# Second-half LRU in the RWKV slots, and two streams of RWKV recurrences in one PSUM bank

## The chip, the cores and the metric

One core of one Trainium2 chip runs the whole program. The metric is the device time of one execution in microseconds (us). Five engines work from queues of their own: TensorE (PE), VectorE (DVE), ScalarE (ACT), GpSimd (POOL) and SyncE (SP). An engine takes its instructions in the order in which they stand in its queue, so an instruction that waits holds up all that is behind it.

## The reference, cut to what matters

One layer of a hybrid recurrent network, for a prompt of 1024 tokens and 8 single-token samples, in float32:

```python
xn = _rmsnorm(x, norm1_g)
P = xn @ w_in                                  # 1024 x 3456, columns split among three groups
o_r, S_r = _rwkv7(...)                         # 6 heads of 64; S = S*diag(w) - ... + v k^T, token by token
o_h, S_h = _hgrn2(...)                         # 6 heads of 64; gated linear attention in chunks of 64
o_l, h_l, c_l = _rglru(...)                    # 256 channels; width-4 convolution, h = a*h + b
x = x + concat([o_r, o_h, o_l]) @ w_out
x = x + square(relu(_rmsnorm(x) @ mlp_w1)) @ mlp_w2
y = _rmsnorm(x)
```

All final states are outputs too. Within `_rwkv7` the last steps are a group norm of each head (mean, variance, scale), a bonus term and a gate.

## The kernel before, in words

Channels lie on the 128 partitions, tokens along the free dimension. The prompt is worked in two halves of 512 tokens (`hf` 0 and 1; the 8 samples ride with half 1).

**The dense products.** Each float32 weight matrix is split into a high and a low part (`wh`, `wl`), and so are the activations (`xh`, `xl`), and a dense tile is 24 matmuls: 8 blocks of 128 rows, three products each. `projections()` is one long generator that makes the dense tiles one after another: the input projection of half 0, tiles `in_...` of 512 tokens, that of half 1 in pieces of 256 and 264, then `out_proj(0)`, `out_proj(1)` and the first part of the MLP. The order of the column blocks is `ORDER`: r, w, l, h are the blocks of RWKV (r, k, v), of its low-rank parts, of the LRU and of HGRN; in half 1 it is `w0 r0 h0 r1 r2 h1 h2 l0 l1`. The up and down products of the MLP come after that and fill the second half of the run.

**The recurrences.** RWKV is worked in 12 parts `q`: a pair of heads `j`, a half `hf`, a quarter `qt` of 256 tokens, that is four chunks of 64 (`PARTS`). A part goes through `rw_operands` (exponentials, transposes), `rw_inverse` (a triangular inverse, matmuls `sc`, `W` and `Y`), `rw_chain` (for each chunk three dependent small matmuls into the tile `ch`, named `pa`, `pu` and `pst` in the code, each read by DVE before the next; at the end 24 small matmuls `po` for the outputs of the part) and `rw_finish` (the group norm on ACT and DVE, then transposes `oT` and the matmul `gate`). HGRN is `hg_run` with its matmuls `hvT`, `hqk`, `gram`, `hkT`, `hS`, `ho`, `hoT`, and for the samples `hsrow`, `hso`, `hsq`; `rw_sample` does the RWKV samples. The LRU is `lru` with the matmuls `lg`.

**What sets the order.** Only PE's order is made by hand. `weave` runs the generators against a planned clock `now`: a generator yields either a number (so many us until its next piece is due; these are the constants D1 to D42) or a key that another one must have set. At each turn the recurrence whose piece is due goes first, and the dense generator fills what is left. The order of the other engines is made by the framework's scheduler, with the priorities of `PRI`.

**Slots.** The projection writes its results into SBUF slots. There are `RPM` = 6 slots "pm" for the r, k, v tiles of RWKV, freed when the operands of the second quarter are done, and `HPM` = 8 slots "hpm" for HGRN (four tiles a block) and the LRU (two tiles a block, `xb` and `gl`). `take` holds the dense generator until a slot is free. The third work tile of the LRU, `lq`, is one buffer of its own. The slots "pm" are taken again by `out_proj`, for the residual tiles `xr` (loaded by POOL's DMA queue) and for squares.

**PSUM banks.** Eight banks: "big" 2 for the dense tiles, "ra" 2 for the inverse, "ch" 1 for the chain and its outputs, "o" 1 shared by all other small products of RWKV and LRU, "h" 2 for HGRN. `bank_o` and `used_o` keep planned time between two uses of "o".

Of the kernel before, what the change touches and what calls it, by code (L numbers as in the profile page):

```python
# [37 lines left out]
L_EV, L_OPS, D1, D2, D3, D4, D5, D6, D7, D8, D9, D10, D11, D12, D13, D14, D15, D16, D17, D18, D19, D20, D21, D22, D23, D24, D25, D26, D27, D28, D29, D30, D31, D32, D33, D34, D35, D36, D37, D38, D39, D40, D41, D42, L_N0, L_RB, L_O = 1.59, 2.88, 3.2, 10.6, 3.9, 1.6, 1.6, 1.6, 6.4, 1.6, 0.5, 1.6, 4.5, 2.08, 2.6, 1.6, 1.6, 1.8, 1.6, 3.8, 8.5, 1.6, 1.5, 3, 1.45, 2, 3, 0.8, 2, 2.6, 4, 4, 4, 1.6, 1.6, 6.31, 1.6, 3.3, 3, 0.99, 9.63, 1.6, 2.2, 1.1, 7.82, 0.54, 1.6  # L38
# [4 lines left out]
PRI = [-100, 0, 0, 300, 300, 300, 100, 300]  # L43
# [9 lines left out]
def kernel(ctx: ExitStack, tc: tile.TileContext, i, o):  # L53
# [397 lines left out]

    def shifted(hf, col, name, out, tag, bufs):
# [3 lines left out]
        pm = rwp.tile([P, HW], F32, tag=tag, name=f"pm_{name}", bufs=bufs)  # L456
# [69 lines left out]
    def rw_operands(q):  # L526
# [49 lines left out]
        G.memset(ee[:, :, 0:1], 1.0)  # L576
        act(ee[:, :, 1:C + 1], ck(t2), AF.Exp)
        act(t1, t2, AF.Exp, scale=-1.0)
        V.tensor_copy(wc, ee[:, :, C])
# [44 lines left out]
    def rw_inverse(q):  # L624
# [7 lines left out]
        sa, ym, xm, mv, kv = (w2(nm, n, u).rearrange("p (u t) -> p u t", t=C) for nm, u in (("sa", 2), ("ym", 3), ("xm", 2), ("mv", 3), ("kv", 3)))  # L632
# [971 lines left out]
```

## Time and profile before

| | us |
|---|---|
| median of 3 timed runs | 1579.41 |
| lowest, highest | 1573.84, 1581.77 |
| the profiled execution, its own time | 1583.56 |
| the profiled execution, first to last instruction (span) | 1581.8 |
| PE busy | 1500.9 |
| DVE, ACT, POOL busy | 757.3, 665.3, 382.5 |

The profile is one execution. "Idle before, releaser" is the time that an engine stood still just ahead of an instruction, and what ended it. A row of the timeline has the start in us, the duration, the engine, the line, the operation, output and inputs, shapes, and the count of like instructions that are merged. Fp32 matmuls whose operands are not split appear as two records each (x16 for 8 matmuls). PE's durations overlap: the pitch of a stream of matmuls is the difference of their starts, not their duration. PEclk is the clock that PE was granted, as a share of full speed.

Up to about 620 us the input projection and the recurrences of both halves run side by side, from about 686 us the first tiles of `out_proj(0)` run beside what is left of the recurrences, and from about 860 us on the MLP has PE to itself.

### The profile page before, as it was taken

What the parts mean: (1) busy time and instruction counts of PE and PEld (TensorE: products, weight loads), DVE (VectorE), ACT (ScalarE), POOL (GpSimd) and SP (SyncE); (2) the same over time, 40 slices, a digit from 0 to 9 for tenths busy, and PEclk for the clock granted to TensorE, in tenths of its full rate; (3) what the DMA queues carried; (4) which work ended last, traced back from release to release, by engine and by line L of the source; (5) the groups of instructions that cost most, each with busy time, mean ns of one, the idle gap of its engine ahead of it and who ended that gap; (6) DMA issues with size and microseconds to landing.
All of it is one profiled execution on the core that took longest, in us unless ns stands there. A gap on an engine that the chain in (4) does not pass through costs nothing.

```text
span 1581.8 us, 31488 instructions
## 1 busy us (share of the span) xinstructions
PE 1500.9 (95%) x13112; PEld 1322.7 (84%) x13112; DVE 757.3 (48%) x1799; ACT 665.3 (42%) x1433; POOL 382.5 (24%) x531
## 2 busy tenths in 40 slices
PE   8989999999998899978999999999999999999997
PEld 6767777888898888866798899889898989988887
DVE  7777866756566665574555222222222222222224
ACT  4544656546544556255434324232332323233232
POOL 4553323224335324323312110101111010101011
PEclk9989999998999999799999999999999999999999
DMA  4334334344434334235442544535344454544242
GB/s 152 125 68 96 84 81 94 79 83 98 91 75 96 74 81 91 62 73 124 119 128 81 107 80 99 102 83 104 83 104 83 102 92 85 102 86 101 47 93 108
DMA packets 53086, 146.98 MB, mean 93 GB/s; under 512 B 6960, under 2 KB 7248, under 8 KB 52944
## 3 DMA queue, kind: packets, MB, share of 16 engines
q0 software_dynamic: 22976, 65.33, 24.9%
q1 hardware_dynamic: 29824, 79.61, 16.1%
q8 instruction: 103, 1.69, 0.5%
q14 instruction: 39, 0.32, 0.1%
q10 hardware_dynamic: 144, 0.04, 0.0%
HBM read 138.87 MB, written 6.07 MB: 92 GB/s over the span
## 4 chain that ended last, share of the span: by engine, by line
PE 72%; DVE 10%; issue 6%; ACT 5%; DMA 4%; POOL 2%; POOLq 0%; SPq 0%; DVEq 0%; ACTq 0%
PE up L76 22%; PE dn L76 19%; PE in L76 13%; PE out L76 4%; PE ch L76 2%; PE W L76 2%; PE Y L76 2%; PE sc L76 1%; PE gram L76 1%; DMA wl_out<-in_w_out 1%; DVE rq L1035 1%; PE ho L76 1%; DMA raw_in<-in_w_in 1%; DMA wl_w<-in_w 1%; ACT gsq L768 1%
## 5 line engine op out<-in xcount | busy, mean ns | idle before, releaser
L76 PE MATMUL in<-xl,wh_in 128*128 128x512 f32 (+3 forms) x648 | 223.4, 345 | 2.1 <-DVE xl L385 2.1
L76 PE MATMUL in<-xh,wh_in 128*128 128x512 f32 (+3 forms) x648 | 223.9, 345 | 0.0
L76 PE MATMUL dn<-hh,wl_w 128*128 128x264 f32 (+2 forms) x696 | 223.2, 321 | 0.3 <-DMA wl_w<-in_w 0.2
L76 PE MATMUL dn<-hh,wh_w 128*128 128x264 f32 (+2 forms) x696 | 222.8, 320 | 0.0
L76 PE MATMUL dn<-hl,wh_w 128*128 128x264 f32 (+2 forms) x696 | 222.7, 320 | 0.0
L76 PE MATMUL in<-xh,wl_in 128*128 128x512 f32 (+3 forms) x648 | 221.4, 342 | 0.5 <-DVE wl_in L293 0.3
L1492 DVE TENSOR_TENSOR mix<-mix,dn 128x512 f32<-128x512 f32 (+2 forms) x192 | 98.4, 512 | 243.4 <-PE dn L76 243.4
L296 POOL DMA_DIRECT2D wl_w<-in_w x86 | 75.2, 877 | 575.4 <-ACT hh L1422 305.9
L291 ACT ACTIVATE wh_w<-raw_w 128x512 fp32r<-128x512 f32 (+1 forms) x90 | 70.7, 785 | 281.6 <-PE dn L76 228.0
L1421 DVE SCALAR_TENSOR_TENSOR rl<-up,rl 128x512 f32<-128x512 f32 (+2 forms) x96 | 49.5, 516 | 204.5 <-ACT rl L1420 204.4
L76 PE MATMUL up<-nxh,wh_w 128*128 128x264 f32 (+1 forms) x512 | 145.9, 285 | 0.1
L76 PE MATMUL up<-nxl,wh_w 128*128 128x264 f32 (+1 forms) x512 | 145.0, 283 | 0.5 <-POOL nxl L1318 0.5
L76 PE MATMUL up<-nxh,wl_w 128*128 128x264 f32 (+1 forms) x512 | 145.3, 284 | 0.0
L76 PEld LDWEIGHTS dn<-hh,wl_w 128*128 128x128 f32 x696 | 130.8, 188 | 14.1 <-DMA wl_w<-in_w 4.4
L76 PEld LDWEIGHTS dn<-hl,wh_w 128*128 128x128 f32 x696 | 130.9, 188 | 10.1
L76 PEld LDWEIGHTS dn<-hh,wh_w 128*128 128x128 f32 x696 | 131.0, 188 | 9.3
L76 PEld LDWEIGHTS in<-xl,wh_in 128*128 128x128 f32 x648 | 127.4, 197 | 13.4 <-DVE xl L385 4.2
L76 PEld LDWEIGHTS in<-xh,wl_in 128*128 128x128 f32 x648 | 127.1, 196 | 11.1 <-issue 1.0
L76 PEld LDWEIGHTS in<-xh,wh_in 128*128 128x128 f32 x648 | 127.3, 196 | 10.6 <-issue 0.7
L1420 ACT ACTIVATE rl<-up 128x512 f32<-128x512 f32 (+2 forms) x96 | 43.3, 451 | 141.0 <-PE up L76 140.9
L76 PE MATMUL up<-nl,wh_w 128*128 128x512 f32 x256 | 101.5, 397 | 0.0
L76 PE MATMUL up<-nh,wl_w 128*128 128x512 f32 x256 | 101.5, 396 | 0.0
(461 smaller groups left out, 3328.3 us busy)
## 6 DMA issues: line engine op xcount, KB each, us to landing
raw_in<-in_w_in SPq DMA_DIRECT2D x53, 512.0 KB, 3.4
wl_in<-in_w_in POOLq DMA_DIRECT2D x43, 512.0 KB, 5.7
raw_w<-in_w SPq DMA_DIRECT2D x32, 512.0 KB, 3.5
raw_w<-in_w SPq DMA_DIRECT2D x64, 256.0 KB, 2.7
wl_w<-in_w POOLq DMA_DIRECT2D x58, 256.0 KB, 4.1
wl_w<-in_w POOLq DMA_DIRECT2D x28, 512.0 KB, 5.6
raw_out<-in_w_out SPq DMA_DIRECT2D x16, 512.0 KB, 3.5
out_y_prompt<-yt SPq DMA_DIRECT2D x16, 256.0 KB, 2.0
```

Of the source, the lines that this page charges most:

```text
L76: PE.matmul(out, lhsT, rhs, start=start, stop=stop)
L291: act(wh[:, ks], raw[:, ks], AF.Copy)
L296: G.dma_start(wl[:, ks], src[:, ks], accum_op=ALU.add)
L768: act(sq, raw[:, g * 64:(g + 1) * 64], AF.Square, bias=sums[:, 0, g:g + 1], accum_out=sums[:, 1, g:g + 1])
L1035: V.tensor_tensor(qp[g][hp, h, :], qef[hp, gc], q[hp, gc], op=ALU.mult)
L1420: act(rl[:, :n], pt[:, :n], AF.Relu)
L1421: V.scalar_tensor_tensor(rl[:, :n], pt[:, :n], 0.0, rl[:, :n], op0=ALU.max, op1=ALU.mult)
L1492: V.tensor_tensor(x2[m][:, c0:c0 + n], x2[m][:, c0:c0 + n], pt[:, :n], op=ALU.add)
```

## The change

- The LRU of half 1 takes its tiles from the slots "pm", after RWKV's r, k and v, and the third work tile (`gq`, before `lq`) is a slot too: three "pm" a block in half 1, three "hpm" a block in half 0.
- `rw_chain` runs as two streams. The pairs (quarter 0 and 1 of one pair of heads) go to them in turn: parts 0, 1, 4, 5, 8, 9 to one, 2, 3, 6, 7, 10, 11 to the other. Each stream has its own `az`, `yz`, `rh`, `ws` and state buffers, and uses its own half of one tile `ch`, made once, in the bank "ch". `bank_ch` and `used_ch` keep 0.9 us of planned time between two chain matmuls of either stream.
- The 24 output matmuls of a part go to a tile `po` in the shared bank "o", held for 3.5 us of planned time, and wait for the previous part's finish before they start, not after.
- To find the room in SBUF: the tile `ee` is gone (`ar` holds the exponentials first and is multiplied in place; a third, shifted Exp per part on ACT), the tile `raw` is gone (the outputs go to one half of `ot`; the scaling is eight DVE instructions of 64 columns in place of four of 128), and `ym` has two buffers in place of three.

```diff
-PRI = [-100, 0, 0, 300, 300, 300, 100, 300]
+PRI = [-100, -100, 0, 0, 300, 300, 300, 100, 300]
...
+    ch_busy = [0.0]
+    def bank_ch():
+        while now[0] < ch_busy[0]:
+            yield ch_busy[0] - now[0]
+    def used_ch():
+        ch_busy[0] = now[0] + L_CH
...
+    def pm_tile(name):
+        return rwp.tile([P, HW + 3], F32, tag="pm", name=name, bufs=RPM)
...
-        G.memset(ee[:, :, 0:1], 1.0)
-        act(ee[:, :, 1:C + 1], ck(t2), AF.Exp)
+        G.memset(ar[:, :, 0, 0:1], 1.0)
+        act(ar[:, :, 1, :], ck(t2), AF.Exp)
         act(t1, t2, AF.Exp, scale=-1.0)
-        V.tensor_copy(wc, ee[:, :, C])
+        act(ar[:, :, 0, 1:C], ck(t2)[:, :, 0:C - 1], AF.Exp)
+        V.tensor_copy(wc, ar[:, :, 1, C - 1])
...
+    chb = ps("ch", "ch")
     def rw_chain(q):
...
         yield ("B", q)
+        if hf == 1 and qt == 0:
+            yield ("C", q - 5)
+        z = q // 2 % 2
+        az, yz = azs[z], yzs[z]
...
-        pt = ps("ch", f"ch_{n}")
-        pa, pu, pst = (pt[:, u * C:u * C + C] for u in range(3))
-        po = pt[:, QT:2 * QT]
+        pa, pu, pst = (chb[:, z * QT + u * C:z * QT + u * C + C] for u in range(3))
...
             if st is not None:
+                yield from bank_ch()
                 mm(pa, az[:, c].rearrange("p h t -> p (h t)"), st)
+                used_ch()
...
             if c == NQ - 1:
+                if q >= 1:
+                    yield ("N", q - 1)
+                po = (yield from bank_o(f"po_{n}"))[:, 0:QT]
                 for c_, h, b, cc in units():
...
-                if q >= 1:
-                    yield ("N", q - 1)
+                used_o(3.5)
...
                 for g in range(NQ):
-                    act(raw[:, g * 64:(g + 1) * 64], po[:, g * 64:(g + 1) * 64], AF.Copy, accum_out=sums[:, 0, g:g + 1])
+                    act(ot[:, g, 0], po[:, g * 64:(g + 1) * 64], AF.Copy, accum_out=sums[:, 0, g:g + 1])
...
         for g in range(NQ):
-            V.tensor_scalar(ot[:, g], bc(raw[:, None, g * 64:(g + 1) * 64], [P, 2, C]), sums[:, 0, g:g + 1], sums[:, 1, g:g + 1],
-                            op0=ALU.add, op1=ALU.mult)
+            for h in (1, 0):
+                V.tensor_scalar(ot[:, g, h], ot[:, g, 0], sums[:, 0, g:g + 1], sums[:, 1, g:g + 1], op0=ALU.add, op1=ALU.mult)
...
-        for w in ("xb", "gl"):
-            yield from take("hpm")
-            x.append(hp_tile(f"l{w}{t}_{hf}"))
-        xb, gl = x
+        for w in ("xb", "gl", "gq"):
+            yield from take("pm" if hf else "hpm")
+            x.append((pm_tile if hf else hp_tile)(f"l{w}{t}_{hf}"))
+        xb, gl, gq = x
...
-        gq = hgp.tile([P, HW], F32, tag="lq", name=f"lq{t}_{hf}", bufs=1)
...
-        free["hpm"] += 2
+        free["pm" if hf else "hpm"] += 3
...
-        weave([each(rw_chain, *NP), each(rw_inverse, *NP[0::2]), ...
+        weave([each(rw_chain, *(x for x in NP if x[0] // 2 % 2 == 0)), each(rw_chain, *(x for x in NP if x[0] // 2 % 2)), each(rw_inverse, *NP[0::2]), ...
```

What the change does to PE's order shows best near the end of half 1's input projection. In the rows, `ch` are chain matmuls, `W` and `Y` those of the inverse, `oT` and `gate` the finish of part 9, `hoT`, `hsrow`, `hso` and `hsq` the end of HGRN's block 1, and `in_1_...` the dense tiles. Before, on PE, the 52 rows that start with the `W` behind the last matmul of block h2 hold no dense matmul; these are the last 10 of them, and the first matmul of block l0 behind them:

```order
L76 MATMUL W_2_1_1_8129<-xm_1_1_7737,sa_1_1_7735 64x64 x8
L76 MATMUL hsrow_8139<-hsdg_8122,bones 128x512
L76 MATMUL ch_1_0_8118<-rh_2_1_0_8126,yz 128x64
L76 MATMUL Y_2_1_1_8146<-ym_1_1_7736,wm_2_1_1_8128 64x64 x8
L81 MATMUL oT_1_1_8157<-ident,ot_1_1_8077 128x128 x4
L76 MATMUL ch_1_0_8118<-mv_1_0_7011,bt_1_0_6811 128x64
L76 MATMUL gate_1_1_8170<-pm_xg_3608,gup 128x256
L76 MATMUL hso_8173<-hq_1_6529,hsst_8120 64x1 x16
L76 MATMUL W_2_1_1_8194<-xm_1_1_7737,sa_1_1_7735 32x32 x8
L76 MATMUL hsq_8205<-hssq_8191,bones 128x8
L76 MATMUL in_1_0_8242<-xh_3295,wh_in_1_7797 128x256
```

In the changed kernel, on PE at the same place, where `hoT` of HGRN's block 1 stands:

```order
L76 MATMUL ch<-st_1_184,az_187 128x64
L76 MATMUL in_1_256_7970<-xh_3268,wh_in_1_7520 128x264
L76 MATMUL in_1_256_7970<-xl_3276,wh_in_1_7520 128x264
L76 MATMUL Y_2_1_1_8024<-ym_1_1_7826,wm_2_1_1_7981 64x64 x8
L81 MATMUL hoT_1_8035<-ident,hot_1_7935 128x128 x4
L76 MATMUL ch<-st_1_1_1_7974,az_186 128x64
L76 MATMUL in_1_256_7970<-xh_3268,wl_in_1_7521 128x264
L76 MATMUL in_1_256_7970<-xh_3269,wh_in_1_7520 128x264
L76 MATMUL in_1_256_7970<-xl_3277,wh_in_1_7520 128x264
L76 MATMUL in_1_256_7970<-xh_3269,wl_in_1_7521 128x264
L76 MATMUL in_1_0_8061<-xh_3262,wh_in_1_7756 128x256
```

The last tile of h2 (`in_1_256_7970`) and the first of l0 (`in_1_0_8061`) now run on between the small matmuls, and l0 no longer stands behind `hsq`. Part 10 (`az_187`) and part 9 (`az_186`), of different streams, have chain matmuls between each other. This is the only longer place where they do: over all 12 parts the stream changes 11 times from one chain matmul to the next, seven of them here. From the last tiles of the input projection on (both kernels start `out_0` at the same row of PE's order, 3280) the two orders have the same pieces at nearly the same rows.

On POOL, the residual tiles `xr` of `out_proj` take "pm" slots. Before, the first two loads stand far ahead, between chain steps of half 1's first pair of heads:

```order
L735 TENSOR_SCALAR ws_0_1_1_6468<-st_0_1_1_6320,wc_1_1_5063 128x64
L736 TENSOR_TENSOR ws_0_1_1_6468<-ws_0_1_1_6468,kv_1_1_5292 128x64
L1260 DMA xr_0_8775<-in_xt 128x512
L861 DMA out_s_wkv<-s_st_6185 128x512
L1260 DMA xr_0_8923<-in_xt 128x512
L735 TENSOR_SCALAR ws_0_1_1_6598<-st_0_1_1_6467,wc_1_1_5063 128x64
```

In the changed kernel, on POOL, the second and third of them stand beside the last chain steps of part 11 (`ws_2_1_1`) and the first LRU output (`out_lru`):

```order
L1003 TENSOR_TENSOR kq_2_1_8980<-kq_2_1_8980,hf_1_7004 128x8x32
L306 DMA wl_out_0_8957<-in_w_out 128x1024
L1284 DMA xr_0_8962<-in_xt 128x512
L758 TENSOR_SCALAR ws_2_1_1_9108<-st_2_1_1_9017,wc_1_1_7591 128x64
L759 TENSOR_TENSOR ws_2_1_1_9108<-ws_2_1_1_9108,kv_1_1_7829 128x64
L1237 DMA out_lru<-lso_8505 128x36
L1284 DMA xr_0_9040<-in_xt 128x512
```

The loads now come after the LRU of half 1 has had the slots; the second one (`xr_0_8962`) waits for a DVE result.

More of the change, by code (lines that the diff above doesn't have):

```diff
@@ L455, in shifted @@
         pr = rwp.tile([P, HT + 16], F32, tag="praw", name=f"praw_{name}", bufs=1)
-        pm = rwp.tile([P, HW], F32, tag=tag, name=f"pm_{name}", bufs=bufs)
+        pm = pm_tile(f"pm_{name}") if tag == "pm" else rwp.tile([P, HW], F32, tag=tag, name=f"pm_{name}", bufs=bufs)
         def evac(pt, c0, n):
@@ L504 @@
     kz = rwp.tile([P, 2, NQ, 2, C], F32, name="kz")
-    az = rwp.tile([P, NQ, 2, C], F32, name="az")
-    yz = rwp.tile([P, NQ, 2, C], F32, name="yz")
+    azs, yzs = ([rwp.tile([P, NQ, 2, C], F32, name=f"{nm}{z}") for z in range(2)] for nm in ("az", "yz"))
     for h in range(2):
-        for z in (kz[brow[1 - h], 0, :, h], kz[brow[1 - h], 1, :, h], az[brow[1 - h], :, h], yz[brow[1 - h], :, h]):
-            G.memset(z, 0.0)
+        for z in (kz[:, 0], kz[:, 1], *azs, *yzs):
+            G.memset(z[brow[1 - h], :, h], 0.0)
     PARTS = [(j, hf, qt) for hf in range(2) for j in range(3) for qt in range(2)]
@@ L631, in rw_inverse @@
         sr = rwp.tile([P, 2, NQ, C], F32, tag="sr", name=f"sr_{n}", bufs=3)
-        sa, ym, xm, mv, kv = (w2(nm, n, u).rearrange("p (u t) -> p u t", t=C) for nm, u in (("sa", 2), ("ym", 3), ("xm", 2), ("mv", 3), ("kv", 3)))
+        sa, ym, xm, mv, kv = (w2(nm, n, u).rearrange("p (u t) -> p u t", t=C) for nm, u in (("sa", 2), ("ym", 2), ("xm", 2), ("mv", 3), ("kv", 3)))
         (S.copy if q < 2 else G.tensor_copy)(ym, bc(id64[:, None, :], [P, NQ, C]))
@@ L763, in rw_finish @@
         om = mix[j][:, hf * HT + qt * QT:hf * HT + qt * QT + QT]
-        ot, raw, sums, bo = (live[q][x] for x in ("ot", "raw", "sums", "bo"))
+        ot, sums, bo = (live[q][x] for x in ("ot", "sums", "bo"))
         V.tensor_scalar(sums[:, 0], sums[:, 0], -1.0 / 64.0, None, op0=ALU.mult)
@@ L767, in rw_finish @@
         for g in range(NQ):
-            act(sq, raw[:, g * 64:(g + 1) * 64], AF.Square, bias=sums[:, 0, g:g + 1],
+            act(sq, ot[:, g, 0], AF.Square, bias=sums[:, 0, g:g + 1],
                 accum_out=sums[:, 1, g:g + 1])
@@ L1250, in evac @@
             else:
-                sq = rwp.tile([P, HW], F32, tag="pm", name=f"sq{m}_{c0}", bufs=RPM)
+                sq = pm_tile(f"sq{m}_{c0}")
                 act(sq[:, :cn], xm, AF.Square)
@@ L1258, in load @@
             ws[m] = next_w(m + 1 < lead or m >= lead)
-            xts[m] = rwp.tile([P, HW], F32, tag="pm", name=f"xr{m}_{hf}", bufs=RPM)
+            xts[m] = pm_tile(f"xr{m}_{hf}")
             nc.gpsimd.dma_start(xts[m][:, :n], i["xt"][m * P:(m + 1) * P, s0:s0 + n])
@@ L1428, in norms @@
     def norms():
-        yield from norm2(*CH[0], lambda nm: rwp.tile([P, HW], F32, tag="pm", name=nm, bufs=RPM))
+        yield from norm2(*CH[0], pm_tile)
         for c in CH[1:]:
@@ L1435 @@
         dense_work = projections()
-        weave([each(rw_chain, *NP), each(rw_inverse, *NP[0::2]), each(rw_inverse, *NP[1::2]), each(rw_operands, *NP), each(rw_finish, *NP), hgrn(),
+        weave([each(rw_chain, *(x for x in NP if x[0] // 2 % 2 == 0)), each(rw_chain, *(x for x in NP if x[0] // 2 % 2)), each(rw_inverse, *NP[0::2]), each(rw_inverse, *NP[1::2]), each(rw_operands, *NP), each(rw_finish, *NP), hgrn(),
                each(lru, *((t, hf) for hf in range(2) for t in range(2)))], dense_work)
```

22 lines of the change are left out of this document (12 added, 10 removed).

## The prediction

> **What bounds the kernel now.** I read the busy times and the 40 slices of the page first, then windows of 20 us, then PE's own timeline where the windows dip, then PE's waits.
>
> ```profile
> span 1581.8 us, 31488 instructions
> PE 1500.9 (95%) x13112; PEld 1322.7 (84%) x13112; DVE 757.3 (48%) x1799; ACT 665.3 (42%) x1433; POOL 382.5 (24%) x531
> PE   8989999999998899978999999999999999999997
> PEclk9989999998999999799999999999999999999999
> ```
>
> PE is the bound: it stands still for 80.9 of 1581.8 us. The change issues the same matmuls, so it can win only where PE stands still or runs at a lower clock. In the second half (the MLP) both are almost absent. The one slice with a clock of 7 is the seventeenth, 633 to 672 us. Windows there (columns: PE, PEld, DVE, ACT, POOL busy, PE's clock, DMA share, GB/s):
>
> ```profile
> 600.00:620.00 20.00, 19.91 (x272) 18.41 (x271) 11.19 (x28) 10.60 (x20) 6.97 (x13) 1.00 0.41 80
> 620.00:640.00 20.00, 15.63 (x252) 12.85 (x250) 11.18 (x34) 9.65 (x45) 11.22 (x15) 0.80 0.35 86
> 640.00:660.00 20.00, 20.00 (x159) 18.27 (x158) 9.26 (x29) 3.26 (x7) 7.24 (x10) 0.68 0.19 44
> 660.00:680.00 20.00, 19.08 (x234) 17.79 (x234) 12.35 (x38) 11.62 (x33) 5.90 (x8) 1.00 0.40 89
> 680.00:700.00 20.00, 17.49 (x180) 14.13 (x179) 18.35 (x40) 12.78 (x27) 5.20 (x7) 1.00 0.18 54
> ```
>
> From 620 to 660 PE stands still for 4.4 us and loses a fifth and a third of its clock. PE's timeline shows what the stretch is made of:
>
> ```profile
> 620.40 0.28 PE L76 MATMUL in<-xh,wl_in 128*128 128x264 f32 x1
> 620.61 0.68 PE L76 MATMUL W<-xm,sa 64*64 64x64 f32 x16
> 621.59 1.15 PE L76 MATMUL ho<-vt,att 64*64 64x64 f32 x32
> 622.66 1.20 PE L76 MATMUL ho<-hst,rq 128*64 128x64 f32 x32
> ...
> 629.54 0.63 PE L81 MATMUL hoT<-ident,hot 128*128 128x128 f32 x4 [1.65 <-DVE gs L765]
> ...
> 642.78 0.59 PE L76 MATMUL hsq<-hssq,bones 128*128 128x8 f32 x2
> 643.23 0.56 PE L76 MATMUL in<-xh,wh_in 128*128 128x256 f32 x1
> ```
>
> No dense matmul runs from 620.6 to 643.2 us, and PE goes from one wait for a small result to the next. The reason is the slots: block h1 holds four "hpm" slots and h2 the other four, so l0 cannot take one until HGRN's block 1 is done, whose last PE piece here is `hsq`. The dense stream, which fills every other wait, is shut out.
>
> **The change part by part.** *The LRU in "pm" slots.* In half 1 the r, k, v of blocks 0 and 1 are used up long before, so l0 finds three free "pm" slots, and PE's new order has dense matmuls through the whole stretch. What that is worth: 22.6 us of small work would cost less between dense tiles at full clock. Prices at full clock, from the chain of waits (start, us) and, for `hso`, PE's timeline:
>
> ```profile
> 560.42 0.61 PE W L76 x16
> 564.74 0.44 PE oT L81 x4
> 572.05 0.49 PE gate L76 x2
> 585.00 1.66 PE ch L76 x46
> 607.45 0.43 PE ch L76 x2
> 751.79 0.86 PE hsrow L76 x2
> 756.17 1.09 PE L76 MATMUL hso<-hq,hsst 64*64 64x1 f32 x32
> ```
>
> From 620.6 on: eight `W` and `Y` groups at 0.61 (4.9, the one behind 620.61 is a pair), the two `ho` rows to 623.79 (2.2), five chain matmuls at 0.43 (2.2), the 24 outputs (1.66), `hoT` and `oT` (0.88), `hsrow` 0.86, `gate` 0.49, `hso` 1.09, `hsq` half of its 0.59 at half clock: 14.5 us. So 8.1 of the 22.6 us are wait and lost clock. Behind it the dense tiles of l0 still run slowly, PE always busy but at a clock of 0.50:
>
> ```profile
> 643.20:652.60 9.40, 9.40 (x56) 9.11 (x57) 4.23 (x15) 0.61 (x2) 4.62 (x5) 0.50 0.10 30
> ```
>
> Of these 9.4 us half, 4.7, are lost. Together 12.8 us. From the windows alone the gain is at most 4.4 us of standing still and 0.20 x 20 + 0.32 x 20 = 10.4 us of clock, 14.8; at least it is the 4.4 us, if the clock falls all the same. I take 12.8.
>
> [...]
>
> *The third LRU tile.* Before, LRU block 1 of half 1 shared `lq` and `xc` with block 0. DVE is busy for 18.35 of the 20 us to 700, and then PE has its longest late wait:
>
> ```profile
> 711.21 1.23 PE L76 MATMUL lg<-lxc,lruw 128*128 128x260 f32 x2 [5.96 <-DVE lxc L1168]
> L1157 DVE TENSOR_TENSOR lq<-lq,lgl x2: 694/696/699, 669.6 to 707.4; 128x520 f32<-128x520 f32 x2
> ```
>
> With `gq` its own slot, the three GELU instructions of block 1 (this one, and two of the same size, one of them lighter: some 1.8 us) stand in DVE's order ahead of block 0's last write, and not behind it. `xc` is still one buffer. Between 0 (they then delay block 0) and 1.8 us; I take 1.
>
> *Two streams of chains.* In the new order the chain ends where it did: the 24 outputs of parts 8 to 11 stand behind nearly the same dense tile, because the operands of part `q` still wait for part `q`-3. The streams alternate 11 times in the run. I take 0; PE's largest wait for the chain bounds the gain:
>
> ```profile
> PE ch L76 <- DVE st L737: 6.4, 12, 1.1
> ```
>
> (us in total, times, longest): at best 6.4 us. At worst each alternation waits for a DVE read of the other half, 11 x 0.53 (6.4 / 12) = 5.8 us.
>
> *The shifted Exp, the smaller scalings, `po` in "o".* ACT gets 12 more Exp of 0.42 us (5.0), DVE four more instructions a part:
>
> ```profile
> L773 DVE TENSOR_SCALAR ot<-raw,gs 128x128 f32<-128x128 f32 x48 | 14.9, 371 | 5.8 <-POOL gs L152 5.8
> L728 DVE COPY mv<-ch 128x64 f32<-128x64 f32 x48 | 10.6, 220 | 20.0 <-PE ch L76 20.0
> L577 ACT ACTIVATE ee<-t x12: 400/418/420, 54.8 to 564.1; 128x256 f32<-128x256 f32 x12
> L751 ACT ACTIVATE raw<-ch 128x64 f32<-128x64 f32 x48 | 10.1, 223 | 15.6 <-PE ch L76 13.8 <-DVE t L590 1.8
> ```
>
> No row has a 64-column scaling; it costs between 0.22 and 0.37 us, nearer the first, which has its width: eight at 0.27 against four at 0.37 is 0.7 us a part, 8 us of DVE in the run. What waits for the scaling is `oT`; that of the last part:
>
> ```profile
> 739.18 0.60 PE L81 MATMUL oT<-ident,ot 128*128 128x128 f32 x4
> 705.74 0.70 DVE L1206 SCALAR_TENSOR_TENSOR mix<-lgl,lxc 128x520 f32<-128x520 f32 x1
> 713.34 0.69 DVE L1246 TENSOR_TENSOR mix<-out,xr 128x512 f32<-128x512 f32 x1 [2.04 <-PE out L76]
> DMA to landing us min/median/max: 2.8/4.0/6.0
> ```
>
> It waits for nothing, dense tiles cover it; with no cover the scalings would cost 0.7 us a part, 8 in all. I count 0.5 us for all of this. The residual tiles `xr` now wait for LRU slots: the second can go out after block 0's last write (to 706.4 here), lands 4 us later (2.8 to 6.0), and is used at 713.3, so some 3 us cover it. Behind it in POOL's queue stand the last chain steps of part 11, which stood behind `out_lru`, and so behind the same write, before.
>
> Sum: 12.8 + 1 + 0 - 0.5 = 13.3 us. Against the profiled execution's own 1583.6 that is 1570.3. That execution lies 4.2 us above the median of 1579.4, so the forecast for the median is 1566.1; I say 1566.
>
> **The rivals.** *The wait moves.* HGRN's block 1 and the RWKV samples are themselves chains of small results, and the dense tiles now run beside them. If these chains were already as fast as DVE, ACT and POOL allow, PE would wait later, at `hvT` or `gram` of block 2. For it: DVE is over 90% busy right behind. Against it: from 600 to 680 DVE is busy for 44.0 of 80 us. It would leave the 4.7 us of clock behind the stretch, or nothing: 1575 to 1579.
>
> *One bank for two streams.* The 5.8 us above come in full: 1566 + 6 = 1572. For it: every chain wait of PE ends with DVE. Against: the planner keeps 0.9 us between them. [...]
>
> *More than the stretch.* If the streams also remove the chain wait (6.4) and `gq` half of the `lg` wait (3.0): 8 to 9 us more than the 1 counted, 1557 to 1558.
>
> *Slower: "o" is held.* A part's outputs now sit in the bank that all transposes of RWKV use, until ACT has read them. Part 9 before, the last output and the end of its reading:
>
> ```profile
> 627.21 0.22 PE L76 MATMUL ch<-vr,sr 64*64 64x64 f32 x1
> 628.31 0.21 ACT L751 ACTIVATION_READ_ACCUMULATOR raw<-ch 128x1 f32 x1
> ```
>
> That is 1.3 us from the start of the one to the end of the other, and 3.5 us are planned. ACT works in order, with all the weight conversions in its queue. If it came 4.2 us late at every part, PE would stand 2 us at the next user of "o", 12 x 2 = 24 us, and the kernel would be 11 us slower, 1590. It decides from 13.3 / 12 = 1.1 us a part on. Against it: ACT is at most 64% busy in these windows.
>
> **How the numbers follow.** Forecast 0.50 (its own range 1561 to 1573, the bounds of its terms); the wait moves 0.17; one bank 0.10; more 0.14; slower 0.09. The time is that of the first, 1566. The range has to leave out no more than 2 in 10: from 1556, the case of more, to 1580, the wait that moves; what is left out is the slower case and the outer ends. A measurement of this kernel can tell 0.5%, 7.9 us: faster is below 1571.5. Of the forecast 0.46 of its 0.50 lie there, all of the case of more, and 0.04 of the others: 0.64. Slower is 0.08, most of the last rival; 0.28 is left for the same.
>
> **What would show it.** [...] It is wrong if waits of `hvT`, `gram`, `s_kk` or of dense tiles for weights grow by as much as the stretch gave, or if waits for "o" (`pw`, `pc_kk`, `vT`, `bt`, `oT`) with ACT as releaser appear at most parts.

## The result, and the profile after

The change is slower: a median of 1585.71 us over 20 runs (1581.94 to 1594.95) against 1578.82 us over 20 runs of the kernel before (1573.70 to 1582.99). The ratio is 1.0057, 95% interval [1.0043, 1.0071], which is 9.0 us (6.8 to 11.2). The forecast was 1566 us, with a range from 1556 to 1580.

The page of the changed kernel (its own time, 1594.95 us, is the highest of its 20):

```profile
span 1593.2 us, 31529 instructions
PE 1504.1 (94%) x13112; PEld 1323.9 (83%) x13112; DVE 766.3 (48%) x1847; ACT 668.5 (42%) x1445; POOL 386.8 (24%) x535
...
PEclk9989999999989999998899999999999999999999
```

PE now stands still for 89.1 us where it stood still for 80.9, and the row of clocks has no 7 at 633 to 672 us any more, but more 8s elsewhere. The windows where the forecast saw its gain:

```profile
600.00:620.00 20.00, 16.67 (x251) 15.19 (x250) 14.96 (x44) 13.46 (x30) 6.51 (x9) 1.00 0.24 54
620.00:640.00 20.00, 19.98 (x321) 18.23 (x321) 10.88 (x33) 9.19 (x34) 7.72 (x11) 1.00 0.33 84
640.00:660.00 20.00, 18.24 (x246) 15.74 (x246) 12.23 (x42) 6.35 (x23) 12.73 (x16) 1.00 0.52 118
660.00:680.00 20.00, 18.53 (x213) 17.19 (x214) 14.04 (x42) 10.33 (x32) 4.92 (x7) 0.91 0.30 71
```

From 620 to 660 us PE works for 38.2 of 40 us at full clock, before for 35.6 at 0.80 and 0.68. The stretch without dense matmuls is gone, and `l0` begins at 636.8 us, ahead of `hsq` at 648.1. So the step that the forecast rests on came in. The loss is elsewhere. PE's waits in the changed kernel (us in total, times, longest):

```profile
PE W L76 <- DVE xm L710: 9.3, 11, 2.4
PE pb_kk L81 <- DVE t L285: 6.1, 4, 2.5
PE out L76 <- DMA wl_out<-in_w_out: 5.9, 2, 3.2
PE lg L76 <- DVE lxc L1192: 5.4, 1, 5.4
...
PE ch L76 <- DVE mv L749: 4.6, 5, 2.0
```

Before, the wait at the head was `ch` for `st` (12 waits of 0.53 us on average, the longest 1.1, 6.4 in all), and `W` waited for `xm` twice:

```profile
PE W L76 <- DVE xm L697: 1.0, 2, 0.6
```

The twelve short waits are gone, and eleven waits of 0.85 us on average have come in their place, the longest 2.4. The windows of the long first stage, 140 to 620 us, show what that does (behind the busy times of PE, PEld, DVE, ACT and POOL stands the clock). Before, then the changed kernel:

```profile
140.00:620.00 480.00, 456.14 (x5875) 402.15 (x5873) 309.38 (x874) 263.62 (x670) 157.56 (x234) 0.98 0.39 85
```

```profile
140.00:620.00 480.00, 451.42 (x5743) 397.39 (x5742) 310.64 (x896) 263.91 (x674) 158.34 (x230) 0.96 0.38 82
```

PE stands still for 28.6 us there, before for 23.9: 4.7 more. The clock falls from 0.98 to 0.96, which over 480 us is some 10 us of PE's speed (0.02 x 480). The sum of the forecast has no term for a new order of PE ahead of 620 us.

### The profile page after: what moved, and what is told of

The parts are those of the page before. It is cut to its first block, busy times and chain, and to the rows that moved or that the text cites. A ratio compares the mean times of both kernels' runs of the same rounds, so it can differ in the third digit from the quotient of the medians.

```text
span 1593.2 us, 31529 instructions
## 1 busy us (share of the span) xinstructions
PE 1504.1 (94%) x13112; PEld 1323.9 (83%) x13112; DVE 766.3 (48%) x1847; ACT 668.5 (42%) x1445; POOL 386.8 (24%) x535
## 4 chain that ended last, share of the span: by engine, by line
PE 68%; DVE 13%; DMA 6%; ACT 6%; issue 5%; POOL 3%; POOLq 0%; SPq 0%; ACTq 0%; DVEq 0%
PE up L76 21%; PE dn L76 19%; PE in L76 13%; PE W L76 2%; PE out L76 2%; PE Y L76 2%; PE ch L76 1%; DVE ot L798 1%; DMA raw_w<-in_w 1%; PE sc L76 1%; DMA wl_out<-in_w_out 1%; DMA raw_out<-in_w_out 1%; PE po L76 1%; PE gram L76 1%; PE ho L76 1%
## 5 line engine op out<-in xcount | busy, mean ns | idle before, releaser
L76 PEld LDWEIGHTS dn<-hh,wl_w 128*128 128x128 f32 x696 | 130.8, 188 | 14.4 <-DMA wl_w<-in_w 5.0
L76 PE MATMUL up<-nh,wh_w 128*128 128x512 f32 x256 | 101.5, 396 | 0.0
```

The lines of the kernel that those rows point to most:

```text
L76: PE.matmul(out, lhsT, rhs, start=start, stop=stop)
```

## The experiments

Eighteen kernels were timed in five groups, each beside the kernel before on the same chip. A ratio is to that kernel; us are (ratio - 1) x 1578. "Same" means that PE's rows are in the order of before, and a number gives the row where the order first differs, the names of buffers left out; the stretch without dense matmuls begins at row 2954 of before. (The change renames buffers, `yz` to `yz0`, from row 415 on; its order first differs at 568.) "Clock" is the mean granted clock over the timed executions.

| run | PE's order | ratio, interval | us | clock |
|---|---|---|---|---|
| (before) | | | | 0.980 |
| ym_two | same | 0.9997 [0.9977, 1.0017] | -0.5 | 0.981 |
| exp_and_scalings | same | 1.0031 [1.0006, 1.0056] | +4.9 | 0.979 |
| lru_alone | other from 2954 | 0.9948 [0.9924, 0.9971] | -8.2 | 0.981 |
| lru_two_slots | as lru_alone | 0.9951 [0.9928, 0.9973] | -7.7 | 0.980 |
| po_in_o | other from 568 | 1.0052 [1.0031, 1.0073] | +8.2 | 0.970 |
| po_short | other from 568 | 1.0059 [1.0037, 1.0081] | +9.3 | 0.974 |
| n_first | other from 765 | 1.0037 [1.0022, 1.0053] | +5.8 | 0.975 |
| detune | other from 525 | 1.0040 [1.0025, 1.0056] | +6.3 | 0.977 |
| detune_down | other from 479 | 1.0061 [1.0038, 1.0085] | +9.6 | 0.975 |
| detune_2 | other from 1219 | 1.0120 [1.0091, 1.0150] | +18.9 | 0.972 |
| lru_on_detuned | as detune, other from 2993 | 0.9994 [0.9978, 1.0010] | -0.9 | 0.978 |
| one_stream | as po_in_o and the change, other from 2955 | 1.0006 [0.9991, 1.0020] | +0.9 | 0.976 |
| one_stream_detune | other from 525 | 1.0068 [1.0042, 1.0094] | +10.7 | 0.974 |
| change_again (the change itself) | other from 568, as po_in_o up to 2955 | 1.0049 [1.0032, 1.0066] | +7.7 | 0.975 |
| change_detune | other from 525 | 1.0060 [1.0037, 1.0082] | +9.5 | 0.974 |
| before_later_lg | other from 3381 | 0.9921 [0.9896, 0.9945] | -12.5 | 0.985 |
| lru_later_lg | as lru_alone to the same block | 0.9895 [0.9870, 0.9921] | -16.6 | 0.985 |
| change_later_lg | as the change, other from 3382 | 0.9975 [0.9958, 0.9992] | -3.9 | 0.979 |

### First group: the parts of the change one by one

**The LRU's slots alone** (lru_alone), the kernel before with:

```diff
-        for w in ("xb", "gl"):
-            yield from take("hpm")
+        for w in ("xb", "gl", "gq"):
+            yield from take("pm" if hf else "hpm")
...
-        gq = hgp.tile([P, HW], F32, tag="lq", name=f"lq{t}_{hf}", bufs=1)
...
-        free["hpm"] += 2
+        free["pm" if hf else "hpm"] += 3
```

> The kernel before with the LRU part of the change alone: half 1's LRU takes three "pm" slots a block, half 0's three "hpm", and the buffer lq is gone. One chain stream, ym in three buffers, po in "ch", as before. Theory A (the slots do what was forecast, and the loss comes from another part of the change): 8 to 13 us faster than before, and between 620 and 660 us a clock of 1.00. Theory B (three "hpm" a block in half 0, or the later residual loads, cost what the stretch gives): within 4 us of before, with the loss between 140 and 360 us or after 680 us.

Measured: 8.2 us faster (4.6 to 12.0). By its time theory A holds. Its windows:

```profile
620.00:640.00 20.00, 19.01 (x305) 17.41 (x306) 12.31 (x35) 11.19 (x46) 9.25 (x12) 1.00 0.39 100
640.00:660.00 20.00, 19.33 (x159) 17.61 (x158) 10.75 (x32) 4.60 (x9) 9.36 (x13) 0.74 0.45 104
```

The first window has the forecast full clock, and PE stands still for 1.0 us there in place of 4.4. The second has not: in this execution the clock is 0.74 there, though PE stands still for 0.7 us only, so the clock that theory A expected did not come.

**Two buffers of `ym`** (ym_two), the kernel before with:

```diff
-("ym", 3)
+("ym", 2)
```

> The kernel before with one number changed: ym has two buffers in place of three. PE's order is the same. Theory A (POOL's copy into ym now waits for the chain two parts back, 25.4 us in 6 waits after the change, and the inverse comes late: W waits 9.3 us for xm after, 1.0 before): 5 to 10 us slower than before, with W waiting for xm 5 us or more in all. Theory B (the waits for ym are covered, W is late because of PE's new order): within 2 us of before.

Measured: -0.5 us (-3.6 to +2.7). Theory A falls. POOL does wait longer for the chain before it writes `ym` (15.7 us in all, before 9.2), but `W` waits for `xm` only 2.2 us in all. This run also gives a second profile of before's order of PE. Its windows at the stretch:

```profile
620.00:640.00 20.00, 15.34 (x262) 12.52 (x258) 9.87 (x32) 7.29 (x40) 12.14 (x16) 0.91 0.35 91
640.00:660.00 20.00, 19.48 (x171) 17.77 (x171) 14.04 (x44) 7.77 (x14) 7.71 (x11) 1.00 0.38 100
...
643.20:652.60 9.40, 9.15 (x67) 7.98 (x66) 8.79 (x25) 2.73 (x5) 3.07 (x6) 1.00 0.49 109
```

PE stands still as long (4.7 us), but the clock is 0.91 and 1.00 where the profile of before had 0.80 and 0.68. The 9.4 us in which the forecast found a clock of 0.50, and from which it took 4.7 us, run at full clock here. In two later profiles with this order of PE, the same window has a clock of 1.00 (before_later_lg) and 0.56 (exp_and_scalings). So the term is there in some executions of this order and not in others.

**The outputs in bank "o"** (po_in_o), the kernel before with:

```diff
-        po = pt[:, QT:2 * QT]
...
             if c == NQ - 1:
+                if q >= 1:
+                    yield ("N", q - 1)
+                po = (yield from bank_o(f"po_{n}"))[:, 0:QT]
                 for c_, h, b, cc in units():
...
-                if q >= 1:
-                    yield ("N", q - 1)
+                used_o(3.5)
```

> The kernel before with one part of the change: the 24 output matmuls of each part go to a tile in the bank "o", held for 3.5 us of planned time, and wait for the previous part's finish before they start. One stream, ym in three buffers, LRU as before. Theory A (the hold of "o" is covered): within 3 us of before, the outputs' waits for st (6.4 us before) smaller. Theory B (the held bank delays the other users of "o"): 6 to 12 us slower, spread over all 12 parts.

Measured: 8.2 us slower (4.9 to 11.5). By the number it is theory B, but not by the profile:

```profile
PE W L76 <- DVE xm L697: 10.0, 9, 2.7
PE out L76 <- DMA wl_out<-in_w_out: 5.9, 3, 2.9
PE ch L76 <- DVE mv L727: 5.3, 4, 1.8
...
PE pc_kk L76 <- ACT t L554: 1.4, 1, 1.4
...
PE ho L76 <- ACT ad L1051: 1.3, 1, 1.3
```

If a held bank delayed its next users, PE would wait at `pw`, `vT`, `bt` or `oT` for ACT's reading of the outputs. No wait of PE names that reading as its releaser, here or in the changed kernel. What has grown is the wait of `W` for `xm` and of `ch` for `mv`, inside the inverse and the chain, and the clock from 140 to 620 us is 0.96 as after the change:

```profile
140.00:620.00 480.00, 453.81 (x5722) 399.60 (x5718) 302.72 (x861) 261.43 (x665) 158.08 (x231) 0.96 0.37 84
...
241.21 1.12 PE L76 MATMUL W<-xm,sa 64*64 64x64 f32 x16 [2.35 <-DVE xm L697]
```

This run says more of the change than its time. Up to row 2955, some 634 us into the run, PE's order here is that of the changed kernel. The two also wait at the same matmuls: `W` for `xm` 2.35 us at 241.2 here and 2.35 at 243.6 there, 1.25 at 315.8 and at 320.5, 2.03 at 452.2 and 2.04 at 457.8, and `ch` for `mv` 1.68 at 192.5 and 2.02 at 194.8. So PE's new order ahead of the stretch comes from the moved outputs alone. The LRU's slots and the second stream change it only from the stretch on. The twelve short waits for `st` are gone here too, with one stream.

**One chain stream** (one_stream), the changed kernel with:

```diff
-        weave([each(rw_chain, *(x for x in NP if x[0] // 2 % 2 == 0)), each(rw_chain, *(x for x in NP if x[0] // 2 % 2)), ...
+        weave([each(rw_chain, *NP), ...
-PRI = [-100, -100, 0, 0, 300, 300, 300, 100, 300]
+PRI = [-100, 0, 0, 300, 300, 300, 100, 300]
```

> The changed kernel with one chain stream that takes the 12 parts in order; buffers, banks and the LRU as in the change. Theory A (the streams hardly alternate and are not the cause): within 3 us of the changed kernel, so 4 to 10 us slower than before. Theory B (chain matmuls of the two streams hold each other up in one bank, or push other work): 5 us or more faster than the changed kernel, so 0 to 5 us faster than before.

Measured: +0.9 us to before, and by the two ratios 8.0 us faster than the change (give or take 3.2). Theory B, by the time. But PE's order is that of the change up to row 2955, and seven of the eleven places where the streams alternate lie right behind; PE's waits for `ch` are not longer with two streams (4.6 + 2.4 us in the changed kernel, 4.4 + 4.1 here).

### Second group: a bank, a wait, or only another order?

**A shorter planned hold** (po_short), po_in_o with the usual 1.6 us:

```diff
-                used_o(3.5)
+                used_o()
```

> The run with the outputs in the bank "o", with one number changed: the planned hold behind the outputs is 1.6 us, as for every other use of that bank, in place of 3.5. Theory A (the long planned hold displaces the other users of "o" in PE's order, and that costs the 8 us): 4 to 9 us faster than with 3.5. Theory B (the outputs' place in "o" costs real waits until ACT has read them): as slow as with 3.5 or slower, with new waits of PE for ACT at vT, bt, pw, pc_kk or oT. Theory C (any new order of PE costs about this much): 4 to 12 us slower than before with waits for DVE at other places.

**The wait for the finish moved ahead, the outputs left in "ch"** (n_first):

```diff
             if c == NQ - 1:
+                if q >= 1:
+                    yield ("N", q - 1)
                 for c_, h, b, cc in units():
...
-                if q >= 1:
-                    yield ("N", q - 1)
```

> The kernel before with one line moved: the outputs of a part wait for the previous part's finish before they start, not after. They stay in the bank "ch". Theory A (the bank causes the loss): within 3 us of before. Theory B (outputs and chain that wait for the finish come late): 5 to 9 us slower, with later chain matmuls of the parts behind. Theory C (any new order of PE costs about this much): 4 to 12 us slower, with waits for DVE at xm, mv or att in place of the outputs' waits for st.

**Only a constant of the plan** (detune), the kernel before with the planned time from `pa` to `pu`:

```diff
-D16 = 1.8
+D16 = 1.9
```

> The kernel before with one planning constant changed, the planned time from pa to pu in the chain, 1.9 us in place of 1.8. Nothing that any engine computes or any bank or buffer changes, only PE's order, in which 1480 of the first 3300 rows then read differently. Theory C (the constants fit one order, and any other order that the planner makes meets the other engines' orders badly): 4 to 10 us slower than before. Theories A and B (bank "o", streams): within 2 us of before.

Measured: po_short +9.3 us, n_first +5.8, detune +6.3 (3.9 to 8.8). The last one says most. It changes no bank, buffer or instruction; it makes the planner lay PE's pieces in another order, and it costs nearly what the moved outputs cost. The text above says that only PE's order changes, and that is not so: the scheduler then orders the other engines anew. In the profiles, DVE's sequence is that of before up to 156 us, and from there on 827 of its 1799 instructions stand at another place. A hold of 1.6 us is no better than one of 3.5. n_first alone would fit theory B as well as C, and its waits of `ch` for `st` stayed (6.4 us), where C expected them to go. So theory C stands as far as these runs go: the constants fit one order, and in the new ones tried here PE's plan and the orders of the other engines, DVE above all, fit worse. The detuned kernel's waits show it in the same place:

```profile
PE W L76 <- DVE xm L697: 5.8, 4, 2.8
```

**The change once more** (change_again):

> The changed kernel itself once more, for a second profile and times beside the other runs of this group. Theory A (the streams' loss is one of order): 6 to 12 us slower than before, and waits over 1.5 us near 194, 243, 440, 458, 755 and 775 us, as in the first profile, since PE's order is fixed. Theory B (the first profile was one bad execution): waits and slow clocks at other places, 740 to 780 us undisturbed.

Measured: 7.7 us slower than before (5.0 to 10.4). The profiled execution took 1583.22 us, 11.7 less than the first, with PE's rows in the same order. The waits of `W` for `xm` are the same (9.2 us, 11 times), as theory A has it; the two waits for the DMA of `wl_out` are shorter (1.4 and 1.7 us, before 3.2 and 2.7), and the slow clocks are partly at other places. One wait shows it. First profile, PE's timeline, then DVE's ahead of it:

```profile
240.22 0.67 PE L76 MATMUL gram<-rql,kq 64*64 64x32 f32 x32
240.82 0.43 PE L76 MATMUL ch<-st,az 128*128 128x64 f32 x2
243.60 1.12 PE L76 MATMUL W<-xm,sa 64*64 64x64 f32 x16 [2.35 <-DVE xm L710]
```

```profile
240.46 0.75 DVE L1004 TENSOR_TENSOR rql<-kq,hq 128x256 f32<-128x256 f32 x1 [1.07 <-ACT kq L1000]
241.14 1.21 DVE L1226 TENSOR_TENSOR_SCAN lxc<-lxb,lgq 128x512 f32<-128x512 f32 x1
242.27 0.27 DVE L706 COPY_PREDICATED ym<-cmask,Y 128x128 f32<-128x128 int32 x1
242.45 0.68 DVE L1230 SCALAR_TENSOR_TENSOR mix<-lgl,lxc 128x512 f32<-128x512 f32 x1
243.05 0.14 DVE L1234 COPY lcar<-lxc 128x1 f32<-128x1 f32 x1
243.12 0.43 DVE L710 STREAM_TRANSPOSE xm<-ym 128x256 f32<-128x256 f32 x1
```

PE's plan puts the next `W` a fixed time behind `Y`. DVE's queue, which is not in that plan, has HGRN's `rql` (itself waiting 1.07 us for ACT) and the scan of the LRU (1.21) in front of `ym`, and the LRU's output (0.68) between `ym` and `xm`. PE waits 2.35 us. Then the clock, windows of 2 us, first profile:

```profile
242.00:244.00 2.00, 0.40 (x8) 0.40 (x10) 2.00 (x7) 0.00 (x0) 1.22 (x2) 0.74 0.00 0
244.00:246.00 2.00, 2.00 (x17) 1.69 (x14) 0.85 (x4) 0.99 (x3) 0.46 (x1) 0.50 0.02 4
246.00:248.00 2.00, 2.00 (x7) 1.61 (x6) 0.86 (x2) 0.81 (x1) 0.27 (x1) 0.50 0.00 0
248.00:250.00 2.00, 2.00 (x19) 1.23 (x19) 0.55 (x3) 1.30 (x2) 1.14 (x3) 0.55 0.28 80
```

and the same wait (2.34 us) in the second profile:

```profile
238.00:240.00 2.00, 0.18 (x2) 0.04 (x1) 2.00 (x5) 0.00 (x0) 1.92 (x2) 1.00 0.03 8
240.00:242.00 2.00, 1.48 (x20) 1.27 (x21) 1.57 (x7) 0.75 (x3) 0.23 (x1) 1.00 0.00 0
242.00:244.00 2.00, 2.00 (x24) 1.47 (x22) 1.49 (x3) 1.59 (x3) 1.00 (x2) 1.00 0.03 8
```

In one execution the wait cost 2.35 us and 3.4 us of PE's speed behind it (0.26 + 0.50 + 0.50 + 0.45 of four times 2 us), in the other 2.34 us alone.

### Third group: luck of an order, or a price of the streams?

The changed kernel (change_detune) and the one-stream kernel (one_stream_detune), both with the edit of detune, `D16` at 1.9:

> The changed kernel with one planning constant changed, the planned time from pa to pu in the chain, 1.9 us in place of 1.8. Nothing computed, no bank and no buffer differs, only PE's order. Theory C (the change pays for its new order, and each order has its own luck): anywhere from 8 us faster to 8 us slower than the changed kernel, and the difference to the same edit with one stream is not the 7 us seen without it. Theory B (two streams cost 7 us whatever the order): within 3 us of the changed kernel, and 5 to 9 us slower than the one stream with the same edit.

> The kernel with one chain stream, and the same planning constant changed, 1.9 us in place of 1.8. Theory B (two streams cost 7 us whatever the order): within 3 us of the one-stream kernel, 5 to 9 us faster than two streams with the same edit. Theory C (luck of the order): its time moves by 3 to 10 us, and so does its distance to two streams.

Measured: change_detune +9.5 us, one_stream_detune +10.7 to before. Two streams and one stream now differ by 1.3 us (give or take 5.4) in the other direction. One edit of 0.1 us in the plan moved the one-stream kernel by 9.8 us (give or take 4.7) and the change by 0.5 (4.2). Theory B falls: the 8 us between change and one_stream (6.8 by the second measurement of the change) are no fixed price of two streams in a bank. What differs besides is PE's order.

**A second constant** (detune_2), the kernel before with:

```diff
-D7 = 6.4
+D7 = 6.6
```

> The kernel before with another planning constant changed, the time planned between the operands' last DVE products and their next PE pieces, 6.6 us in place of 6.4. Theory C (before's constants fit its one order): 4 to 10 us slower than before, as with the first constant (6.3 us by the medians). Rival (the first constant was special, since it moves the chain): within 2 us of before.

Measured: 18.9 us slower (14.4 to 23.7), far past theory C's 4 to 10, in its direction. Two of its waits, before 6.1 and 2.1 us:

```profile
PE pb_kk L81 <- DVE t L275: 10.6, 6, 3.2
...
PE ch L76 <- DVE mv L728: 7.2, 5, 1.9
```

**A later `lg`** (lru_later_lg), lru_alone with:

```diff
-        yield D39
+        yield D39 + 8 * (t and hf)
```

> The LRU part of the change alone, and the last LRU block's four lg matmuls planned 8 us later, so that dense tiles fill the 5.1 us in which PE waits for lxc there. PE's order is the same up to that block. If that wait costs what it shows and the slow clock behind it: 4 to 8 us faster than the LRU part alone, so 12 to 16 us faster than before. If the chain of DVE work behind it sets the end of this stage (lg, the LRU's output, the dense tiles of k = 7): within 2 us of the LRU part alone.

Measured: 16.6 us faster than before (12.5 to 20.5), 1561.01 us median, 8.4 faster than lru_alone (give or take 5.5). This kernel beats both of the case. The wait of lru_alone ends at 700.0 us. The window behind it, 700 to 720 us, in lru_alone and then in this one:

```profile
700.00:720.00 20.00, 20.00 (x167) 16.16 (x168) 11.05 (x26) 11.36 (x17) 4.47 (x8) 0.85 0.46 108
```

```profile
700.00:720.00 20.00, 17.53 (x183) 14.45 (x182) 11.29 (x27) 11.34 (x23) 5.45 (x9) 1.00 0.60 138
```

The wait of `lg` for `lxc` (5.1 us in lru_alone) is no longer among its waits, and the slow clock behind it is gone too.

### Fourth group: are the gains their own?

**The slots on another order** (lru_on_detuned): the edits of detune and of lru_alone together.

> The kernel before with the planned time from pa to pu at 1.9 us (6.3 us slower than before by the medians) and with the LRU part of the change. PE's order is that of the detuned kernel up to the end of half 1's HGRN block 1. If the gain of the slots is the stretch's own: 5 to 11 us faster than the detuned kernel, so within 5 us of before. If it was luck of one order: within 3 us of the detuned kernel, 4 to 9 us slower than before.

Measured: -0.9 us to before, so by the two ratios 7.2 us (give or take 3.5) faster than the detuned kernel whose order it shares up to row 2993. The slots are worth 7 to 8 us on both orders, within these intervals.

**Without the third tile** (lru_two_slots), lru_alone with:

```diff
-        for w in ("xb", "gl", "gq"):
+        for w in ("xb", "gl"):
...
+        gq = hgp.tile([P, HW], F32, tag="lq", name=f"lq{t}_{hf}", bufs=1)
...
-        free["pm" if hf else "hpm"] += 3
+        free["pm" if hf else "hpm"] += 2
```

> The LRU part alone without its third tile: half 1's LRU takes two "pm" slots a block, half 0's two "hpm", and the third work tile is the shared buffer lq, as before. PE's order is that of the LRU part alone, row for row. The prediction gave the third tile 1 us (0 to 1.8): within 2 us of the LRU part alone, 7 to 9 us faster than before, with a wait of lg for lxc of 5 to 7 us. If the shared buffer holds up the second block more than that: 3 us or more slower than the LRU part alone.

Measured: 7.7 us faster than before, 0.5 less than with the third tile, inside both intervals. `lg` waits 5.5 us for `lxc`, with the third tile 5.1.

**The later `lg`** in the kernel before (before_later_lg) and in the changed one (change_later_lg), with the edit of `D39` above:

> The kernel before, with the last LRU block's four lg matmuls planned 8 us later and nothing else changed. PE's order is the same up to there. If the wait of 5.96 us at lg is what the later lg saves: 6 to 11 us faster than before. If the gain needs the LRU's slots (its dense tiles ahead): within 3 us of before.

> The changed kernel, with the last LRU block's four lg matmuls planned 8 us later. If the wait of 5.4 us at lg is saved here as in the LRU part alone: 6 to 11 us faster than the changed kernel, so 1577 to 1580 us, the time of before. If the later streams or residual loads end last there: within 3 us of the changed kernel.

Measured: before_later_lg 12.5 us faster (8.7 to 16.4); change_later_lg 3.9 us faster than before, and by the ratios 11.6 (give or take 3.8) faster than the change. The waits themselves are 6.0 and 5.4 us, so the gain is about twice the wait. A slow clock goes with it, 0.83 in this window before and 1.00 in before_later_lg:

```profile
700.00:720.00 20.00, 13.29 (x112) 10.17 (x111) 11.03 (x31) 9.54 (x13) 4.98 (x9) 0.83 0.51 115
```

```profile
700.00:720.00 20.00, 19.18 (x206) 15.77 (x207) 10.81 (x33) 10.64 (x40) 7.84 (x10) 1.00 0.52 132
```

The median of change_later_lg, 1574.66 us, is 2.3 us below what was expected of it.

### Fifth group: the added DVE work, and the other side of the constant

**The third Exp and the eight scalings alone** (exp_and_scalings), the kernel before without `ee` and `raw`:

```diff
-        act(ee[:, :, 1:C + 1], ck(t2), AF.Exp)
+        act(ar[:, :, 1, :], ck(t2), AF.Exp)
+        act(ar[:, :, 0, 1:C], ck(t2)[:, :, 0:C - 1], AF.Exp)
...
-            V.tensor_scalar(ot[:, g], bc(raw[:, None, g * 64:(g + 1) * 64], [P, 2, C]), ...
+            for h in (1, 0):
+                V.tensor_scalar(ot[:, g, h], ot[:, g, 0], ...
```

> The kernel before with the SBUF savings in the operands and the finish alone: no tile ee (a third, shifted Exp on ACT), no tile raw (eight DVE scalings of 64 columns in place of four of 128). PE's order is that of before, row for row. The prediction counted 0.5 us for them: within 2 us of before. If the longer finish comes late at oT and gate: 3 to 8 us slower, with waits of PE at oT or gate at most parts.

Measured: 4.9 us slower (0.9 to 8.8), with PE's order unchanged. The scaling of 64 columns takes 0.323 us on average, that of 128 took 0.371 (before, in the rows of the prediction):

```profile
L773 DVE TENSOR_SCALAR ot<-ot,gs 128x64 f32<-128x64 f32 x96 | 25.3, 323 | 4.1 <-POOL gs L152 4.0
```

96 of them take 25.3 us where 48 of the wide ones took 14.9. At `oT` PE waits for them 0.8 us in all (2 waits). They come ahead of `ym` and `xm` in DVE's queue, at 636 us, in the stretch without dense work:

```profile
PE pb_kk L81 <- DVE t L275: 9.5, 4, 3.3
...
PE W L76 <- DVE xm L697: 6.2, 4, 4.1
...
634.26 1.20 DVE L773 TENSOR_SCALAR ot<-ot,gs 128x64 f32<-128x64 f32 x5 [0.48 <-POOL gs L152]
635.38 0.28 DVE L693 COPY_PREDICATED ym<-cmask,Y 128x128 f32<-128x128 int32 x1
635.58 0.53 DVE L773 TENSOR_SCALAR ot<-ot,gs 128x64 f32<-128x64 f32 x2
...
636.38 0.43 DVE L697 STREAM_TRANSPOSE xm<-ym 128x256 f32<-128x256 f32 x1
...
636.96 1.12 PE L76 MATMUL W<-xm,sa 64*64 64x64 f32 x16 [4.11 <-DVE xm L697]
```

In three other profiles with this order of PE, `W` waits for `xm` 1.0, 2.2 and 1.9 us in all, and `pb_kk` for `t` 6.1, 6.2 and 7.7. At this place the scalings stood behind `xm` before (632.90 us, `xm` at 631.99), so the scheduler's order of DVE has changed here too, with PE's order the same. So the first wait is the scalings' doing; the growth of the second is hardly clear of its scatter. In the changed kernel the same stretch is covered, so this part's share of the loss may be smaller there; that was not measured apart.

**The constant lowered** (detune_down), the kernel before with:

```diff
-D16 = 1.8
+D16 = 1.7
```

> The kernel before with the planned time from pa to pu in the chain at 1.7 us in place of 1.8. Nothing but PE's order changes. If before's constants fit one order and any other costs: 4 to 18 us slower, as with 1.9 (6 us) and with the other constant (17 us). If only longer planned times cost (PE's pieces pushed later): within 3 us of before, or faster.

Measured: 9.6 us slower (6.0 to 13.4). Both directions of this constant cost, and so did the other constant. The constant `D39` is the exception: a longer one for the last LRU block won 8 to 13 us. So before's constants are not the best in every place; only a small shift of the two others, which reorders most of the recurrences, cost each time.

## Why the prediction was wrong

**The stretch, 12.8 us: right in mechanism, too large.** It measured 8.2 (4.6 to 12.0), and 7.2 on another order. The step "of these 9.4 us half, 4.7, are lost" failed: the clock of 0.50 behind the stretch is there in some executions (0.50, 0.56) and not in others (1.00 twice). Over all timed executions the clock is 0.980 before and within 0.001 of that with the slots, so hardly any of the slots' gain is clock; what is left is packing, dense tiles in the waits between the small matmuls. The forecast also took the 4.2 us by which the profiled execution lay above the median off the sum, though the slow clock in the stretch is part of what made that execution long, so part of it was counted twice. The lower bound of the step, 4.4, and its upper bound, 14.8, hold the result. The profiled execution of before had a mean clock of 0.972, 0.008 under the mean of its kind, which was not to be seen from one profile.

**The third tile, 1 us:** 0.5, within the noise. `lg` waits for `lxc` with it (5.1 us) as without it (5.5).

**Two streams, 0 us: not contradicted.** The distance to one stream was -8.0 us under one set of constants and +1.3 under another. PE's waits for `ch` fell from 10.5 us (6.4 + 2.1 + 2.0) to 7.0 (4.6 + 2.4), but the moved outputs had already brought them to 7.9 with one stream (po_in_o, 5.3 + 2.6). The rival "one bank" (a wait of 0.53 us at each of 11 alternations) has no wait in the profiles of the change that speaks for it.

**"I count 0.5 us for all of this": the step that failed.** It priced the Exp, the scalings and the outputs in "o" by their instructions, and looked for their wait at one user, `oT`. The Exp and scalings alone cost 4.9 us (0.9 to 8.8), above all by delaying `xm` in DVE's queue (`W` waits 6.2 us for it, 4.1 of them up to 636.96 us). The outputs with their earlier wait cost 8.2 (4.9 to 11.5) as a kernel of their own, and they are what gives the change its new order of PE from row 568 to row 2955, with the long waits for `xm` and `mv` and the clock of 0.96. The whole budget speaks of the stretch and of what lies behind it; what another order costs ahead of the stretch has no term in the sum. Six kernels with the LRU as before and another order of PE ahead of the stretch lie 5.8 to 18.9 us above before, three of them by a changed constant alone.

**The rival "slower: o is held"** (1590, chance 0.09) came near the time and had the wrong mechanism: it looked for 2 us at every part, and no wait of PE in po_in_o or in the changed kernel has ACT's reading of the outputs as its releaser (po_short has one, of 0.4 us at `bt`); the shorter hold did not help. Its number was right by accident. **"The wait moves"** had the right idea at the wrong place: it looked for new waits at `hvT` and `gram` of block 2, and they came at `W`, at `ch` for `mv` and at `hoT` from 190 us on.

**The signs in the profile after:** `l0` begins before `hsq` (636.8 and 648.1 us), and from 600 to 680 us the longest time from the start of one dense matmul to that of the next is 4.9 us, before 22.8; both are as the forecast needs them. `lg` waits 5.4 us, and the waits for `ch` are 7.0 in all. The clock is 1.00 from 560 to 660 us and 0.91 in the window behind (660 to 680). PE's idle time is 89.1 us, before 80.9, where the forecast needs less; this is the sign that spoke.

**The sum as measured:** the slots -8.2, the Exp and scalings +4.9, the moved outputs +8.2, `ym` -0.5 make +4.4 for the change with one stream, which measured +0.9 (-1.4 to 3.2); each term has an interval of about 3 to 4 us either way. The change itself is at +7.7 to +9.0; its order differs from that of one_stream behind row 2955 only, and which of its pieces there costs the difference is open. How much of the 8.2 is a price of the outputs' new place and how much is any new order's cannot be told from these runs: no kernel had the outputs in "o" and the old order. Whether constants fitted anew to the change would bring it to the 8 us of the slots was not tried.

## What to carry to other kernels

Where one engine's order is planned by constants fitted to it, price a change that alters the order by first measuring a neutral perturbation of the constants: here 0.1 us in one of them cost 6 to 10 us, where the change was to win 13. Test the parts with the order held still (same rows on the planned engine), and add the ones that stand. Then look for the single longest wait of the bound engine: moving four matmuls 8 us later in the plan won 8.4 to 12.5 us on each of three kernels, while the whole restructuring lost 8 to 9.

## What the runs showed of the hardware

Executions of one kernel differ by the clock. Over 28 runs of before in the first group (1569.52 to 1586.32 us) the time goes with the granted clock (correlation -0.80), 10.7 us for 0.01 of mean clock; in the runs of before in the other four groups the correlation is -0.73 to -0.87. In the profiles of before and of the change, in windows of 0.4 us, the clock falls to 0.50 at 14 and at 20 places. But for the last one of each, which reaches to the end of the program, such a fall lasts 3.4 us (1.7 us of loss) or a multiple of it: before 3.4 us six times, 6.8 six times and 20.5 once (632.1 to 652.7), after 3.4 us thirteen times, 6.8 five times and 10.2 once. The fall at the wait of 2.35 us above is one of 6.8 us (243.0 to 249.8), and in the other execution of the same program the clock is 1.00 at that wait.

Twelve waits of 0.53 us on average (the waits of `ch` for `st` before) went with a clock of 0.98 to 0.99 from 140 to 620 us in two profiles of that order; eleven waits for `xm` of up to 2.4 us, beside others, with 0.96 in two profiles of the change. That long waits cost more clock than short ones is not shown by this. In detune PE stands still for 31.5 us in that stretch, more than in the change (28.6), with waits of up to 3.7 us, and the clock is 0.98:

```profile
140.00:620.00 480.00, 448.51 (x5788) 393.37 (x5784) 310.11 (x872) 261.56 (x666) 155.77 (x230) 0.98 0.36 83
```

What sets the clock's falls, no run here tells.
